# A decoder layer on one core: block products of the second MLP product alternate with tiles of the first, and weight sums are made by adding DMAs

## The chip, the core and the metric

The kernel runs on one core of one Trainium2 chip. The metric is the device time of one launch in microseconds (us), the median of the runs of a kernel; lower is better. Five engines work side by side: TensorE (PE, with its weight loads PEld), VectorE (DVE), ScalarE (ACT), GpSimd (POOL) and SyncE (SP), which here only issues DMAs. Each works through its own instructions in order; semaphores tie them together.

## What is computed

One layer over 512 positions of width 1024, in float32: a sparse attention branch and a latent attention branch, gates, an output projection, and then the MLP, which is all that the change touches:

```python
        x = x + merged @ w_out[l]
        h2 = rmsnorm(x, mlp_norm_g[l])
        x = x + jnp.square(jax.nn.relu(h2 @ w_ff1[l])) @ w_ff2[l]
    return rmsnorm(x, final_norm_g)
```

`w_ff1` is 1024 x 4096 and `w_ff2` 4096 x 1024.

## The kernel before, in words

Every float32 operand of a product is split in a high part `hi` (float32r, a Copy on ACT) and a rest `lo` (a subtraction on DVE); a product is three matmuls, hi·hi, lo·hi and hi·lo (`mm3`, L141 to L143).

**First product.** The 4096 hidden columns are cut into 32 tiles of 128. `ff1(f)` makes one tile for all 512 tokens: 8 x 3 = 24 matmuls of 512 columns into one PSUM bank, then Relu (L910) and Square (L911) on ACT into `z`. Its weights come from DRAM by SP (L112, tile `wraw`), and are split by `pre` (whi L119 on ACT, wlo L121 on DVE).

**Second product.** The hidden rows go in 8 groups `g` of 512, four ff1 tiles each. Within a group the product of z (transposed) and `w_ff2` is taken as a 2 x 2 block product in the manner of Strassen and Winograd, with seven block products in place of eight. The blocks A of z are 256 tokens by 256 hidden rows, the blocks B of the weights 256 hidden rows by 512 columns; S1 to S4 are sums of blocks of A, T1 to T4 sums of blocks of B. `ORDER` names the seven operand pairs and their order. One block product is a **pair** of units (m = 0, 1: 128 tokens each); a unit is 6 matmuls into one PSUM bank `pl` (four banks, `psL`), and then DVE adds the bank into `acc` (the result), `U` or `V` (sums that several blocks share), L979.

- The blocks B11, B12, B22, B21 of a group are loaded by SP into `wraw` (L918, `raws`), the same four buffers that the ff1 weights use.
- T1 to T4 (L944) and S1 to S4 (L929 to L935) are made on POOL, one tensor operation each.
- `put_a` splits an A operand into tile `as` (ACT L953, DVE L954), `put_b` a B operand into tile `b` (ACT L960, DVE L961), which has `NBS` = 6 buffers: a pair's buffer is free once its 12 matmuls are done, and `puts(g, k)` then fills it with the operand six pairs on.

**Order.** PE's order is that of the code. For each group it runs the four ff1 tiles of the next group in a row (21.8 us by the trace), and then the seven pairs of this group in a row. The other engines' instructions are placed by a scheduler. `finish` and `final` (L1001 to L1065) turn the sums of the last group into the output: sums on POOL and DVE, squares on ACT, the row factor `r` on POOL, and the scaled rows by ACT and DVE, in an order that `ff2` gives for the last group.

Of the kernel before, what the change touches and what calls it, by code (L numbers as in the profile page):

```python
# [49 lines left out]
def body(nc, tc, ctx, a, out, dbg=lambda name, ap: None):  # L50
    pe, dve, act, pool, sp = nc.tensor, nc.vector, nc.scalar, nc.gpsimd, nc.sync
# [19 lines left out]
    def utile(i, dt, name):  # L71
        return u_p.tile([128, 4, S], dt, tag=f"u{i}", name=name)
# [98 lines left out]
    k = 0  # L171
    for nk in (1, 1, 2, 2, 2):
# [3 lines left out]
        for kk in range(k, k + nk):  # L176
# [3 lines left out]
            else:  # L180
# [4 lines left out]
                                     op0=ALU.mult, op1=ALU.subtract)  # L185
            cs = [slice(128 * j, 128 * j + 128) for j in range(3)]
# [142 lines left out]
    for j in range(3):  # L329
# [9 lines left out]
        if j == 1:  # L339
# [12 lines left out]
            for j in range(2):  # L352
                t = t_p.tile([128, S], F32, tag="s2k", name="iqf", bufs=4)
# [523 lines left out]
    for b in range(NB):  # L877
# [10 lines left out]
    Z, AS, BS, RAW, TT, SS = {}, {}, {}, {}, {}, {}  # L890
# [21 lines left out]

    def raws(g):
        for key in ("B11", "B12", "B22", "B21"):
            j, n = int(key[1]) - 1, int(key[2]) - 1
            r = wr_p.tile([128, 1024], F32, tag="wraw", name="wraw").rearrange("p (q d) -> p q d", q=2)
            rows = slice((4 * g + 2 * j) * 128, (4 * g + 2 * j + 2) * 128)
            sp.dma_start(r, a["wff2"][rows, 512 * n:512 * n + 512].rearrange("(q p) d -> p q d", p=128))  # L918
            RAW[g, key] = r
# [18 lines left out]
    def operand_b(g, key):
        if key[0] == "B":
            return RAW[g, key]  # L940
        if (g, key) not in TT:
            t = TT[g, key] = wt_p.tile([128, 2, 512], F32, tag="t", name=key, bufs=3)
            x, y = {"T1": ("B12", "B11"), "T2": ("B22", "T1"), "T3": ("B22", "B12"), "T4": ("B21", "T2")}[key]
# [12 lines left out]

    def put_b(g, k):
        x = operand_b(g, ORDER[k][1])
        t = bs_p.tile([128, 2, 2, 512], F32R, tag="b", name="b", bufs=NBS)
        act.activation(t[:, 0], x, AF.Copy)  # L960
        dve.tensor_tensor(t[:, 1], x, t[:, 0].bitcast(F32), op=ALU.subtract)  # L961
        BS[g, k] = (t[:, 0], t[:, 1])

    BLOCK = {0: (0, 0), 3: (0, 1), 4: (0, 0), 5: (1, 1), 6: (1, 0)}

    def unit(g, k, m, cuts=(0, 512)):
        p = pl_tile()
        ah, al = AS[g, "op", k]
        bh, bl = BS[g, k]
        ms = slice(m * 128, (m + 1) * 128)  # L970
        for lo, hi in zip(cuts, cuts[1:]):
            c = slice(lo, hi)
            mm3(p[:, c], [(ah[:, q, ms], al[:, q, ms], bh[:, q, c], bl[:, q, c]) for q in range(2)])
            i, n = BLOCK.get(k, (0, 0))
            b = 2 * i + m
            cs = slice(512 * n + lo, 512 * n + hi)

            def add(t):
                dve.tensor_tensor(t, p[:, c], t, op=ALU.add)  # L979

            def first(t):
                if g == 0:
                    act.activation(t, p, AF.Copy)
                else:
                    add(t)

            if k in BLOCK:
                add(acc[:, b, cs])
            if k == 0:
                first(U[:, m])  # L990
            elif k == 1:
                add(U[:, m])
            elif k == 2:
                first(V[:, m])
            if g == NG - 1:
                finish(k, m, b, n, cs)

    def finish(k, m, b, n, cs):
        c12, c21, c22 = acc[:, m, 512:], acc[:, 2 + m, :512], acc[:, 2 + m, 512:]
        if k == 1:  # L1000
            pool.tensor_tensor(c21, c21, U[:, m], op=ALU.add)  # L1001
        elif k == 2:
            pool.tensor_tensor(V[:, m], U[:, m], V[:, m], op=ALU.add)  # L1003
            pool.tensor_tensor(c12, c12, V[:, m], op=ALU.add)  # L1004
        elif k == 5:
            pool.tensor_tensor(c21, c21, c22, op=ALU.add)
            dve.tensor_tensor(c22, c22, V[:, m], op=ALU.add)  # L1007
        if k >= 3:
            final(b, n, cs)

    def puts(g, k):
        n = NP * g + k + NBS
        if n < NP * NG:
            put_b(*divmod(n, NP))
        if g + 1 < NG and (k % 2 or k == NP - 1):
            for kk in range(k - k % 2, min(k - k % 2 + 2, NP)):
                put_a(g + 1, kk)

    def ff2(g):
        if g + 1 < NG:  # L1020
            raws(g + 1)
        if g < NG - 1:
            for k in range(NP):
                for m in range(2):
                    unit(g, k, m)
                puts(g, k)
        else:
            for k in range(NP - NBS):
                for m in range(2):
                    unit(g, k, m)  # L1030
                puts(g, k)
            for m in range(2):
                for k in range(NP - NBS, NP):
                    unit(g, k, m, (0, 256, 512) if m and k == NP - 1 else (0, 512))
# [57 lines left out]
    for g in range(NG):  # L1092
        if g + 1 < NG:
            for j in range(4):
                ff1(4 * (g + 1) + j)
        if g == NG - 2:
            uo = [utile(4 + i, F32, f"o{i}") for i in range(4)]
            fo = [uo[b // 2][:, 2 * (b % 2):2 * (b % 2) + 2].rearrange("p a b -> p (a b)") for b in range(NB)]
            gf = uo[2][:, 0:2].rearrange("p a b -> p (a b)")
            xf = [uo[2][:, 2], uo[2][:, 3], uo[3][:, 0], uo[3][:, 1]]  # L1100
            sp.dma_start(gf, bc(a["gfin"], [128, D]))
# [49 lines left out]
```

## Time and profile before

| | before |
|---|---|
| median of 3 runs | 749.47 us (748.76 to 751.18) |
| the profiled execution's own time | 748.43 us |
| its span, first to last instruction | 746.7 us |
| mean granted TensorE clock | 0.982 |
| busy: PE, DVE, ACT, POOL | 93%, 74%, 49%, 40% |

A row of the timeline gives the start, the duration, the engine, the line, the operation with its tiles, and, in brackets, how long the engine had stood idle and what released it. Matmuls follow each other every 0.227 us at full clock although each lasts 0.39, since they overlap; how fast PE goes is therefore read from starts. A stretch is described by the busy time of each engine in it. The MLP takes from about 371 us to the end of the span.

### The profile page before, as it was taken

To read this page: it belongs to the slowest core of one execution; us is meant where nothing else is said; L and a number is where in the kernel's file an instruction comes from. 1 tells how busy PE (TensorE), PEld (TensorE's weight loads), DVE (VectorE), ACT (ScalarE), POOL (GpSimd) and SP (SyncE) were. 2 spreads that over 40 slices of the span, in tenths; PEclk is the share of its full clock that TensorE was granted. 3 is DMA by queue.
4 is the path that set the end of the run, shared out by engine and by line. 5 is a ranking of instruction groups with operands and counts; after the bars stand their busy time and mean duration, and the time that the engine had idled before them with its cause. 6 is when DMAs were issued, how large, how long until landed. Compare 5 with 4: busy or idle time off the path is not lost. (4 is left out here: it accounts for less than half of the span.)

```text
span 746.7 us, 10090 instructions
## 1 busy us (share of the span) xinstructions
PE 696.4 (93%) x3653; PEld 559.2 (75%) x3654; DVE 555.1 (74%) x920; ACT 364.0 (49%) x630; POOL 301.2 (40%) x276
## 2 busy tenths in 40 slices
PE   9999999999999999999989989898998989989791
PEld 7879788678666678888878868686776868768571
DVE  6587899999999746753387775949679395892985
ACT  5566777645545455621265634435344353443332
POOL 2314596743355412300434615225151351534544
PEclk9999999999999999999999999999999999999996
DMA  8532531122311159830052231332322314221003
GB/s 312 208 107 86 148 114 43 43 85 84 115 43 44 44 174 334 285 110 0 1 198 86 85 114 57 106 98 78 116 84 85 112 56 141 84 85 57 0 1 113
DMA packets 30050, 77.18 MB, mean 103 GB/s; under 512 B 3568, under 2 KB 4464, under 8 KB 30000
## 3 DMA queue, kind: packets, MB, share of 16 engines
q1 hardware_dynamic: 29136, 75.45, 30.4%
q10 hardware_dynamic: 864, 1.08, 0.4%
q8 instruction: 29, 0.48, 0.3%
q14 instruction: 21, 0.17, 0.1%
HBM read 69.31 MB, written 6.29 MB: 101 GB/s over the span
## 5 line engine op out<-in xcount | busy, mean ns | idle before, releaser
L121 DVE TENSOR_TENSOR wlo<-wraw,whi 128x1024 fp32r<-128x1024 f32 (+1 forms) x60 | 86.0, 1437 | 56.8 <-ACT whi L119 56.1
L141 PE MATMUL pl<-b,as 128*128 128x512 f32 (+1 forms) x226 | 91.2, 404 | 34.2 <-DVE acc L979 26.5
L119 ACT ACTIVATE whi<-wraw 128x1024 fp32r<-128x1024 f32 (+1 forms) x71 | 74.7, 1052 | 98.4 <-PE pl L142 61.3
L143 PE MATMUL pl<-h2h,wlo 128*128 128x512 f32 (+1 forms) x280 | 104.7, 374 | 2.9 <-DVE wlo L121 2.9
L141 PE MATMUL pl<-h2h,whi 128*128 128x512 f32 (+1 forms) x280 | 104.9, 375 | 0.3 <-ACT h2h L874 0.3
L142 PE MATMUL pl<-h2l,whi 128*128 128x512 f32 (+1 forms) x280 | 104.6, 373 | 0.3 <-DVE h2l L875 0.3
L143 PE MATMUL pl<-b,as 128*128 128x512 f32 (+1 forms) x226 | 90.0, 398 | 0.0
L142 PE MATMUL pl<-b,as 128*128 128x512 f32 (+1 forms) x226 | 89.5, 396 | 0.0
L944 POOL TENSOR_TENSOR T<-wraw 128x1024 f32<-128x1024 f32 x16 | 42.2, 2634 | 101.2 <-DMA wraw<-wff 101.2
L979 DVE TENSOR_TENSOR acc<-pl,acc 128x512 f32<-128x512 f32 (+1 forms) x81 | 52.4, 674 | 40.0 <-PE pl L143 37.0
L141 PEld LDWEIGHTS pl<-b,as 128*128 128x128 f32 x226 | 43.7, 193 | 49.2 <-ACT as L953 17.8
L143 PEld LDWEIGHTS pl<-h2h,wlo 128*128 128x128 f32 x280 | 53.1, 190 | 12.5 <-DVE wlo L121 3.3
L142 PEld LDWEIGHTS pl<-h2l,whi 128*128 128x128 f32 x280 | 53.3, 190 | 9.9 <-DVE h2l L875 0.5
L141 PEld LDWEIGHTS pl<-h2h,whi 128*128 128x128 f32 x280 | 53.3, 190 | 9.8 <-ACT h2h L874 0.5
L944 POOL TENSOR_TENSOR T<-wraw,T 128x1024 f32<-128x1024 f32 x16 | 42.5, 2654 | 42.1 <-DVE b L961 24.0
L960 ACT ACTIVATE b<-T 128x1024 fp32r<-128x1024 f32 x32 | 33.7, 1057 | 45.2 <-PE pl L143 44.9
L143 PEld LDWEIGHTS pl<-b,as 128*128 128x128 f32 x226 | 43.6, 193 | 9.2
L142 PEld LDWEIGHTS pl<-b,as 128*128 128x128 f32 x226 | 43.8, 194 | 8.7
L714 DVE TENSOR_SCALAR oh<-posbc,thr 128x400 bf16<-128x400 f32 (+31 forms) x128 | 46.1, 412 | 3.5 <-PE pl L735 3.5
L595 POOL TENSOR_SCALAR pra<-pra,rs 128x400 f32<-128x400 f32 (+31 forms) x32 | 34.4, 1082 | 35.2 <-DVE rs L594 35.1
L237 PE MATMUL pl<-hh,whi 128*128 128x512 f32 x112 | 44.7, 399 | 0.0
L961 DVE TENSOR_TENSOR b<-wraw,b 128x1024 fp32r<-128x1024 f32 x24 | 43.2, 1802 | 1.4 <-ACT b L960 1.2
(307 smaller groups left out, 1654.5 us busy)
## 6 DMA issues: line engine op xcount, KB each, us to landing
wraw<-wff SPq DMA_DIRECT2D x64, 512.0 KB, 3.6
wraw<-wF SPq DMA_DIRECT2D x24, 512.0 KB, 3.3
gd<-gt SPq DMA_DIRECT2D x16, 256.0 KB, 2.2
wraw<-wbr SPq DMA_DIRECT2D x8, 512.0 KB, 4.2
wraw<-wout SPq DMA_DIRECT2D x8, 512.0 KB, 5.7
gx<-gd SPq DMA_DIRECT2D x16, 256.0 KB, 3.2
xtok<-x SPq DMA_DIRECT2D x4, 512.0 KB, 10.9
acc<-x SPq DMA_DIRECT2D x1, 2048.0 KB, 9.5
```

What stands on the lines that cost most here:

```text
L119: act.activation(hi, raw, AF.Copy)
L121: eng.tensor_tensor(lo, raw, hi.bitcast(F32), op=ALU.subtract)
L141: pe.matmul(ps, lh, rh, start=(i == 0), stop=False)
L142: pe.matmul(ps, lh, rl, start=False, stop=False)
L143: pe.matmul(ps, ll, rh, start=False, stop=(i == n - 1))
L237: pe.matmul(p, h[:, k], hh[k], start=(k == 0), stop=False)
L595: pool.tensor_scalar(pr, pr, rs, None, op0=ALU.mult)
L714: dve.tensor_scalar(oh[:, :n], posbc[:, :n], thr[:, 4 * G + q:4 * G + q + 1], None, op0=ALU.is_le)
L944: pool.tensor_tensor(t, operand_b(g, x), operand_b(g, y), op=ALU.subtract)
L960: act.activation(t[:, 0], x, AF.Copy)
L961: dve.tensor_tensor(t[:, 1], x, t[:, 0].bitcast(F32), op=ALU.subtract)
L979: dve.tensor_tensor(t, p[:, c], t, op=ALU.add)
```

## The change

**PE's order.** In a group the seven pairs are no longer in a row. Where a digit is a pair and a letter an ff1 tile of the next group, the order is now `0 a 1 2 b 3 4 c 5 d 6`. The ff1 tiles use the two banks of `psT` (`pt`), so the four banks of `psL` are left to the pairs. The operand pairs stand in another order (A12·B21 is second, S3·T3 sixth), and U gets its second part from pair 3.

**Weight sums.** T1 to T4 are not made by POOL's arithmetic. SP loads one source block from DRAM into the tile, and then POOL issues a second DMA that adds the other block to it (`accum_op`), from DRAM for T1 and T3, from the tile of T3 or T2 for T2 and T4. So that only additions are needed, the T's have other signs, and so have S1, S4 and the sums in `unit` and `finish`. The blocks B11, B21, B22 that are used as they are go into their own tile `raw` (3 buffers), T into `t` (3 buffers) and `b` has 5 buffers.

**Placement of the rest.** `load(g + 1, i)` comes after pair i, `put_b` five pairs ahead, `put_a` of the next group's first operand after tile b, of the next five after tile d, of the last after pair 6. In the last group pairs 0 and 1 run whole, then units 2 to 6 for m = 0, then for m = 1. The scaling of the final gain is on ACT.

```diff
-    ORDER = (("A11", "B11"), ("S2", "T2"), ("S1", "T1"), ("S4", "B22"), ("A12", "B21"), ("S3", "T3"),
+    ORDER = (("A11", "B11"), ("A12", "B21"), ("S1", "T1"), ("S2", "T2"), ("S4", "B22"), ("S3", "T3"),
              ("A22", "T4"))
-    NBS = 6
+    NBS = 5
...
-            p = pl_tile()
+            p = pt_tile().rearrange("p a b -> p (a b)")
             ff1_mm(p, f)
...
+    def raw(g, key):
+        r = RAW[g, key] = wt_p.tile([128, 2, 512], F32, tag="raw", name=key, bufs=3)
+        sp.dma_start(r, wsrc(g, key))
+
+    def tsum(g, key):
+        t = TT[g, key] = wt_p.tile([128, 2, 512], F32, tag="t", name=key, bufs=3)
+        x, y = {"T1": ("B11", "B12"), "T3": ("B12", "B22"), "T2": ("B11", "T3"), "T4": ("B21", "T2")}[key]
+        sp.dma_start(t, wsrc(g, x))
+        pool.dma_start(t, TT[g, y] if y[0] == "T" else wsrc(g, y), accum_op=ALU.add)
+
+    LOADS = ((raw, "B11"), (raw, "B21"), (tsum, "T1"), (tsum, "T3"), (tsum, "T2"), (raw, "B22"), (tsum, "T4"))
...
-                pool.tensor_tensor(t, z0[:, :, t1], z1[:, :, t1], op=ALU.add)
+                pool.tensor_tensor(t, z0[:, :, t1], z1[:, :, t1], op=ALU.subtract)
...
-            pool.tensor_tensor(t, operand_b(g, x), operand_b(g, y), op=ALU.subtract)
...
+    def pair(g, k):
+        for m in range(2):
+            unit(g, k, m)
         n = NP * g + k + NBS
         if n < NP * NG:
             put_b(*divmod(n, NP))
...
+    def group(g):
+        for step in "0a1 2b3 4c5 d6 ":
+            if step.isdigit():
+                pair(g, int(step))
+                load(g + 1, int(step))
+            elif step != " ":
+                ff1(4 * (g + 1) + "abcd".index(step))
+            if step == "b":
+                put_a(g + 1, 0)
+            if step == "d":
+                for k in range(1, 6):
+                    put_a(g + 1, k)
+        put_a(g + 1, 6)
+
+    def last_group(g):
+        for k in range(2):
+            pair(g, k)
+        for m in range(2):
+            for k in range(2, NP):
+                unit(g, k, m, (0, 256, 512) if m and k == NP - 1 else (0, 512))
...
-            pool.tensor_scalar(gf, gf, float(D) ** 0.5, None, op0=ALU.mult)
+    act.activation(gf, gf, AF.Copy, scale=float(D) ** 0.5)
```

In the rows below a name with a number is one tile: S_5930 one of the S, T_5967 one of the T, z_5871 the second half of a group's z. First POOL, around the sums S of one middle group. Before, two weight sums, three S, the third weight sum, the fourth S and the last weight sum:

```order
L944 TENSOR_TENSOR T_5552<-wraw 128x1024
L944 TENSOR_TENSOR T_5551<-wraw,T_5552 128x1024
L929 TENSOR_TENSOR S_5530<-z_5373,z_5440 128x512
L931 TENSOR_TENSOR S_5529<-S_5530,z_5373 128x512
L935 TENSOR_TENSOR S_5580<-z_5440,S_5529 128x512
L944 TENSOR_TENSOR T_5645<-wraw 128x1024
L933 TENSOR_TENSOR S_5625<-z_5373 128x512
L944 TENSOR_TENSOR T_5813<-wraw,T_5551 128x1024
```

Now, with T3, T2 and T4 of this group and T1 of the next group (T_6070) ahead of the four S of this group:

```order
L927 DMA T_5815<-wff 128x2x512
L927 DMA T_5837<-T_5815 128x1024
L927 DMA T_5967<-T_5837 128x1024
L927 DMA T_6070<-wff 128x2x512
L944 TENSOR_TENSOR S_5931<-z_5714,z_5871 128x512
L946 TENSOR_TENSOR S_5935<-S_5931,z_5714 128x512
```

The four tensor operations T became four DMA issues, and the last of them, which belongs to the group after, stands ahead of the S that this group's third pair needs.

Second DVE at the same place, where a group's operands are split while its first pair runs. Before, `as` pairs stand between the additions of single block products:

```order
L979 TENSOR_TENSOR acc<-pl,acc 128x512 x2
L961 TENSOR_TENSOR b<-T_5552,b 128x1024
L954 TENSOR_TENSOR as<-S_5530,as 128x512
L954 TENSOR_TENSOR as<-S_5580,as 128x512
L979 TENSOR_TENSOR acc<-pl,acc 128x512 x2
```

Now (pair 6 of the group before is added around S_5931, pair 0 of this group after all five):

```order
L960 TENSOR_TENSOR as<-z_5871,as 128x512
L960 TENSOR_TENSOR as<-S_5931,as 128x512
L989 TENSOR_TENSOR acc<-pl,acc 128x512
L968 TENSOR_TENSOR b<-B_5893,b 128x1024
L960 TENSOR_TENSOR as<-S_5935,as 128x512
L960 TENSOR_TENSOR as<-S_5940,as 128x512
L960 TENSOR_TENSOR as<-S_5944,as 128x512
L960 TENSOR_TENSOR as<-z_5871,as 128x512
L989 TENSOR_TENSOR acc<-pl,acc 128x512
L995 TENSOR_TENSOR U<-pl,U 128x512
L989 TENSOR_TENSOR acc<-pl,acc 128x512
L995 TENSOR_TENSOR U<-pl,U 128x512
```

What empties the banks of pair 0 now stands behind the splits of S2, S4, S3 and A22.

## Rows read from the trace of the kernel before

**Rows 1.** The page: span and busy time of each engine.
```profile
span 746.7 us, 10090 instructions
PE 696.4 (93%) x3653; PEld 559.2 (75%) x3654; DVE 555.1 (74%) x920; ACT 364.0 (49%) x630; POOL 301.2 (40%) x276
```

**Rows 2.** Timeline of ACT: the Relu of two successive ff1 tiles, and the splits.
```profile
448.73 0.58 ACT L910 ACTIVATE z<-pl 128x512 f32<-128x512 f32 x1
449.33 0.63 ACT L911 ACTIVATE z<-z 128x512 f32<-128x512 f32 x1
...
454.17 0.58 ACT L910 ACTIVATE z<-pl 128x512 f32<-128x512 f32 x1
...
464.31 1.06 ACT L960 ACTIVATE b<-wraw 128x1024 fp32r<-128x1024 f32 x1 [1.60 <-PE pl L143]
465.27 0.61 ACT L953 ACTIVATE as<-z 128x512 fp32r<-128x512 f32 x1
```

**Rows 3.** Stretches: from:to and length, busy time (count) of each engine, clock, DMA share, GB/s.
```profile
432.45:478.79 46.34, 43.01 (x181) 34.81 (x181) 33.07 (x35) 19.67 (x26) 15.99 (x8) 0.96 0.28 91
478.79:523.49 44.70, 41.37 (x181) 33.63 (x181) 33.04 (x35) 19.67 (x26) 16.37 (x8) 1.00 0.29 94
...
659.22:705.64 46.42, 41.35 (x180) 33.62 (x181) 32.59 (x33) 17.05 (x23) 21.42 (x9) 1.00 0.16 57
```

**Rows 4.** Timeline of PE, the rows where it had stood idle, and one more start.
```profile
384.40 0.50 PE L143 MATMUL pl<-h2h,wlo 128*128 128x512 f32 x1 [2.90 <-DVE wlo L121]
...
432.45 0.50 PE L141 MATMUL pl<-b,as 128*128 128x512 f32 x1 [3.09 <-DVE acc L979]
...
478.79 0.47 PE L141 MATMUL pl<-b,as 128*128 128x512 f32 x1 [2.57 <-DVE acc L979]
...
705.64 0.47 PE L141 MATMUL pl<-b,as 128*128 128x512 f32 x1 [2.58 <-DVE acc L979]
...
710.05 0.40 PE L141 MATMUL pl<-b,as 128*128 128x512 f32 x1
```

**Rows 5.** Timeline of DVE in the pairs of one group.
```profile
465.40 3.20 DVE L961 TENSOR_TENSOR b<-wraw,b 128x1024 fp32r<-128x1024 f32 x1 [0.20 <-ACT b L960]
468.53 0.68 DVE L954 TENSOR_TENSOR as<-z,as 128x512 fp32r<-128x512 f32 x1
...
473.44 1.21 DVE L961 TENSOR_TENSOR b<-T,b 128x1024 fp32r<-128x1024 f32 x1
474.58 3.46 DVE L954 TENSOR_TENSOR as<-S,as 128x512 fp32r<-128x512 f32 x2
477.96 1.28 DVE L979 TENSOR_TENSOR acc<-pl,acc 128x512 f32<-128x512 f32 x2
```

**Rows 6.** Timeline of POOL in the same group.
```profile
461.58 1.31 POOL L931 TENSOR_TENSOR S<-S,z 128x512 f32<-128x512 f32 x1
...
465.13 2.39 POOL L944 TENSOR_TENSOR T<-wraw 128x1024 f32<-128x1024 f32 x1
469.95 1.29 POOL L933 TENSOR_TENSOR S<-z 128x512 f32<-128x512 f32 x1 [2.43 <-DVE as L954]
474.73 2.76 POOL L944 TENSOR_TENSOR T<-wraw,T 128x1024 f32<-128x1024 f32 x1 [3.49 <-DVE b L961]
```

**Rows 7.** The page: DMA issues, with count, size and median us to landing.
```profile
wraw<-wff SPq DMA_DIRECT2D x64, 512.0 KB, 3.6
...
xtok<-x SPq DMA_DIRECT2D x4, 512.0 KB, 10.9
acc<-x SPq DMA_DIRECT2D x1, 2048.0 KB, 9.5
```

**Rows 8.** Timeline of DVE and POOL in the last group.
```profile
684.74 2.78 POOL L1102 TENSOR_SCALAR o<-o 128x1024 f32<-128x1024 f32 x1 [10.25 <-DMA o<-gfin]
...
713.62 0.68 DVE L979 TENSOR_TENSOR acc<-pl,acc 128x512 f32<-128x512 f32 x1
...
740.28 0.42 DVE L979 TENSOR_TENSOR acc<-pl,acc 128x256 f32<-128x256 f32 x1 [0.70 <-PE pl L143]
```

More of the change, by code (lines that the diff above doesn't have):

```diff
@@ L911, in ff1, with wsrc, load @@
         act.activation(z, z, AF.Square)
[L913 to L919, printed above, removed]
+    def wsrc(g, key):
+        j, n = int(key[1]) - 1, int(key[2]) - 1
+        rows = slice((4 * g + 2 * j) * 128, (4 * g + 2 * j + 2) * 128)
+        return a["wff2"][rows, 512 * n:512 * n + 512].rearrange("(q p) d -> p q d", p=128)
+    def raw(g, key):
[7 more added lines that the diff above has]
+    LOADS = ((raw, "B11"), (raw, "B21"), (tsum, "T1"), (tsum, "T3"), (tsum, "T2"), (raw, "B22"), (tsum, "T4"))
+    def load(g, i):
+        if g < NG:
+            f, key = LOADS[i]
+            f(g, key)
     def operand_a(g, key):
-        z0, z1 = Z[g, 0], Z[g, 1]
+        z0, z1 = Z.get((g, 0)), Z.get((g, 1))
         t0, t1 = slice(0, 256), slice(256, 512)
@@ L934, in operand_a @@
             else:
-                pool.tensor_tensor(t, z1[:, :, t0], operand_a(g, "S2"), op=ALU.subtract)
+                pool.tensor_tensor(t, z1[:, :, t0], operand_a(g, "S2"), op=ALU.add)
         return SS[g, key]
[L938 to L943, printed above, removed]
-            pool.tensor_tensor(t, operand_b(g, x), operand_b(g, y), op=ALU.subtract)
-        return TT[g, key]
     def put_a(g, k):
@@ L957, in put_b @@
     def put_b(g, k):
-        x = operand_b(g, ORDER[k][1])
+        key = ORDER[k][1]
+        x = (RAW if key[0] == "B" else TT)[g, key]
         t = bs_p.tile([128, 2, 2, 512], F32R, tag="b", name="b", bufs=NBS)
@@ L962, in put_b @@
         BS[g, k] = (t[:, 0], t[:, 1])
-    BLOCK = {0: (0, 0), 3: (0, 1), 4: (0, 0), 5: (1, 1), 6: (1, 0)}
+    BLOCK = {0: (0, 0), 1: (0, 0), 4: (0, 1), 5: (1, 1), 6: (1, 0)}
     def unit(g, k, m, cuts=(0, 512)):
@@ L976, in unit @@
             cs = slice(512 * n + lo, 512 * n + hi)
[L978 to L983, printed above, removed]
-                else:
[L985 to L994, printed above, removed]
+            if k in BLOCK:
+                t = acc[:, b, cs]
+                if k == 5:
+                    dve.tensor_tensor(t, t, p[:, c], op=ALU.subtract)
+                else:
+                    dve.tensor_tensor(t, p[:, c], t, op=ALU.add)
+            t = {0: U, 2: V, 3: U}.get(k)
+            if t is not None:
+                if g == 0 and k != 3:
+                    act.activation(t[:, m], p, AF.Copy)
+                else:
+                    dve.tensor_tensor(t[:, m], p[:, c], t[:, m], op=ALU.add)
             if g == NG - 1:
@@ L999, in finish @@
         c12, c21, c22 = acc[:, m, 512:], acc[:, 2 + m, :512], acc[:, 2 + m, 512:]
-        if k == 1:
+        if k == 3:
             pool.tensor_tensor(c21, c21, U[:, m], op=ALU.add)
-        elif k == 2:
-            pool.tensor_tensor(V[:, m], U[:, m], V[:, m], op=ALU.add)
-            pool.tensor_tensor(c12, c12, V[:, m], op=ALU.add)
+            pool.tensor_tensor(V[:, m], U[:, m], V[:, m], op=ALU.subtract)
+            pool.tensor_tensor(c12, c12, V[:, m], op=ALU.subtract)
         elif k == 5:
-            pool.tensor_tensor(c21, c21, c22, op=ALU.add)
-            dve.tensor_tensor(c22, c22, V[:, m], op=ALU.add)
-        if k >= 3:
+            pool.tensor_tensor(c21, c21, c22, op=ALU.subtract)
+            dve.tensor_tensor(c22, c22, V[:, m], op=ALU.subtract)
+        if k in (1, 4, 5, 6):
             final(b, n, cs)
-    def puts(g, k):
+    def pair(g, k):
+        for m in range(2):
+            unit(g, k, m)
         n = NP * g + k + NBS
@@ L1014, in puts @@
             put_b(*divmod(n, NP))
[L1015 to L1034, printed above, removed]
+    def group(g):
[17 more added lines that the diff above has]
+                unit(g, k, m, (0, 256, 512) if m and k == NP - 1 else (0, 512))
     parts = {b: 0 for b in range(NB)}
@@ L1083, in body @@
     V = z_p.tile([128, 2, 512], F32, name="V")
-    pool.tensor_tensor(acc[:, 2:4, :512], acc[:, 2:4, :512], acc[:, 2:4, 512:], op=ALU.subtract)
-    raws(0)
+    pool.tensor_tensor(acc[:, 2:4, :512], acc[:, 2:4, :512], acc[:, 2:4, 512:], op=ALU.add)
+    for i in range(NP):
+        load(0, i)
     for j in range(4):
@@ L1091, in body @@
             put_b(0, k)
[L1092 to L1101, printed above, removed]
-            pool.tensor_scalar(gf, gf, float(D) ** 0.5, None, op0=ALU.mult)
-        ff2(g)
+    for g in range(NG - 1):
+        group(g)
+    uo = [utile(4 + i, F32, f"o{i}") for i in range(4)]
+    fo = [uo[b // 2][:, 2 * (b % 2):2 * (b % 2) + 2].rearrange("p a b -> p (a b)") for b in range(NB)]
+    gf = uo[2][:, 0:2].rearrange("p a b -> p (a b)")
+    xf = [uo[2][:, 2], uo[2][:, 3], uo[3][:, 0], uo[3][:, 1]]
+    sp.dma_start(gf, bc(a["gfin"], [128, D]))
+    act.activation(gf, gf, AF.Copy, scale=float(D) ** 0.5)
+    last_group(NG - 1)
     ff_st.close()
```

## The prediction, made before the changed kernel had run

> **What bounds the kernel now.** I read the page first: PE is busy 93% of a span of 746.7 us [rows 1], but busy time of overlapping matmuls hides gaps, so I took PE's pace from starts. The Relu of two successive ff1 tiles starts 5.44 us apart [rows 2], which is 24 matmuls at 0.227 us. A pair, 12 matmuls, is then 2.72 us, and a group of four tiles and seven pairs 4 x 5.44 + 7 x 2.72 = 40.8 us. Next the stretches from one long idle of PE to the next: there are six of one group each between 432.45 and 705.64 us, two of 46.3 us, one of 46.4 and three of 44.7 (three stand there) [rows 3]. The difference is lost time, and the idle rows of PE say who ends it: DVE's additions into `acc` [rows 4]. In the seven pairs in a row a pair needs a bank every 1.36 us, and DVE has 33 us of work per group [rows 3], most of it there: splits of `b` at 1.2 us that stretch to 3.2 while POOL works on T, and pairs of `as` splits that take 3.46 in place of 1.28 [rows 5, 6]. The bound is DVE's queue within the pairs, not its 33 us in 40.8. After a long idle of PE the clock falls in some groups: 0.96 mean beside 1.00, and the stretch is 46.3 in place of 44.7 [rows 3].
>
> Against the work at 0.227 us per matmul, the profiled execution loses, to the start of the last group:
> - From the late `wlo` of ff1 tile 3 to 432.45 [rows 4]: the wait ends at 384.40 and is 2.90 long, so work would go on at 381.50. It holds 22 matmuls of the tile, four tiles and six pairs, 5.0 + 21.8 + 16.3 = 43.1 of 50.95: **7.9 lost**.
> - The six groups: 705.64 − 432.45 = 273.2 for 6 x 40.8 = 244.8: **28.4 lost**.
> - The last pair of group 6, 705.64 to 710.05 at the low clock: 4.4 for 2.7, **1.7 lost**.
>
> Together 38.0. The last group takes the rest, from 710.05 to the end: 36.7.
>
> **What the change does to each term.** *Interleaving.* Two pairs in a row are now the longest run; between them PE has 5.44 us in `pt` banks, which ACT empties. In a group DVE adds 16 banks, 0.64 each, splits seven `b` (1.21) and seven `as` (0.68) and four weights (about 1.2): 10.2 + 8.5 + 4.8 + 4.8 = 28.3 of 40.8 [rows 5]. Per pair it is at most four additions and one split, 3.8, with tiles between. So the 28.4 and the 1.7 go, unless something new is late. Its place can be read in the order: DVE splits S1, S2, S4, S3 and A22 ahead of the additions of pair 0, and pair 2 needs pair 0's banks. That is the new edge.
>
> *How long that edge holds.* Let t = 0 be the start of pair 0. The last tile of z is done at −2.72, Relu and Square bring z to −1.5 [rows 2]. If POOL begins S1 at s, S1, S2, S4 and S3 follow at 1.3 each, and take turns with DVE's splits where both read from memory [rows 5, 6]; after two such turns the last S ends near s + 7.1, its split on ACT and DVE and that of A22 (0.6 + 0.7 + 0.7) near s + 9.6, the first bank of pair 0 is free 1.3 later, at s + 10.9. Pair 2 is due at 2.72 + 5.44 + 2.72 = 10.9. So s may be 0 without loss, and from there every microsecond is PE's.
>
> *What sets s.* T1 of the next group is added by a DMA that POOL issues ahead of S1. Its buffer was T2's, which T4 reads. So: `put_b` of T1 runs after pair 4, which ends at −16.3, and its DVE half ends at −14.0 (1.06 + 1.21) [rows 2, 5]; SP's load for T4, 3.6 [rows 7], lands at −10.4; the add takes X, from POOL's issue to landing; SP's load for T1, 3.6, lands at X − 3.2 − 3.6 = X − 6.8; POOL issues the add, about 1.0. Hence s = X − 5.8, not under −1.5.
>
> *X.* The trace has no DMA from POOL and none that adds. Nearest rows: a plain load of 512 KB lands after 3.6, one of 2 MB after 9.5 [rows 7]. That is 1.97 per 512 KB and 1.6 fixed. An add has the old contents to read as well, so I count 512 KB twice: 1.6 + 3.9 = 5.5, and 0.5 for POOL's issue and for other loads in flight: **X = 6.0**. Below, 3.6 (the add for nothing); above, 9.5 to 10.9, the slowest rows of that view. The Trainium skill, in DMA: Bandwidth & Descriptors, Anatomy of one DMA — SWDGE (gpsimd) path, fits a POOL DMA by 2.0 us plus bytes over 436 GB/s, and Collectives: The Full Stack, The bandwidth ceiling, says that an adding DMA is slow not for the addition but for its two source reads; by both, X would be an estimated 2.0 + 2 x 1.2 = 4.4, and the sum below 6 us lower. No run here shows that.
>
> With X = 6.0, s = 0.2; I add 0.8, since four further DMAs of 512 KB per group make loads land later than 3.6: **1.0 per group, six groups, 6.0**.
>
> There is a second loop: `put_b` of T3 waits for those additions; then load 3.6, add X, the add of T2, the add of T4, load 3.6, issue 1.0, and from s to the end of `put_b` of T3 10.9 + 1.3 + 1.2 = 13.4. That is 21.6 + 3X, and exceeds 40.8 from X = 6.4 on. From there a group costs 3 us for every microsecond of X.
>
> *T sums off POOL.* Four operations, 2.4 to 2.8 each [rows 6], leave POOL; what they hid behind was DVE, and they return what they took from it (3.2 against 1.21). This is inside the 28.4 already.
>
> *Start.* ff1 weights no longer share buffers with B, so tile 3 does not wait for `wlo`, and group 0 is interleaved as well: the 7.9 go. New: ACT's split of T2 stands ahead of z's last Square, and T2 needs two adds in a row. The loads begin near 371; T3's, the fourth, lands near 371 + 1.6 + 4 x 1.97 = 380.5, so with X = 6 T2 is there at 392.5. Its split (1.06 and 1.21), the Square and A12's split (0.63, 0.61, 0.68) take 4.2, to 396.7, and pair 1 is due at 381.5 + 5.44 + 2.72 + 5.44 = 395.1. I count **1.5**, and 2 per microsecond of X.
>
> *Last group.* Its additions began at 713.62, 3.6 after its first matmul [rows 8], and DVE and POOL, not PE, set the rest. Now they begin at s + 9.6, and the scaling of the gain, now on ACT, stands ahead of z's last Square; POOL got that gain after 10.25 of waiting at 684.74 [rows 8], a microsecond after the last tile. So they begin some 6 later, and one `b` split more (1.2) falls in; the units of m = 1 are one fewer after the two whole pairs, from which I take 3 back: **4.4 longer**, with bounds 1 and 8.
>
> **Sum.** 748.4 − 38.0 + 6.0 + 1.5 + 4.4 = 722.3 for the profiled execution; the median of the runs is 1.0 above it, so 723.3, rounded to **723**.
>
> **Rivals.**
> - *A cheap add.* X is 3.6 to 5: no edge is reached, start and groups lose nothing, the last group's additions begin 1.5 sooner: 749.5 − 38.0 + 2.9 = 714. For it: POOL's queue is nearly empty. Against: it would read as cheap as a plain load.
> - *Half a gain.* X is 7 to 8.2, the second loop binds at 21.6 + 3 x 7.4 = 43.8, 3.0 per group: 749.5 − 38.0 + 18 + 4.3 + 4.4 = 738.
> - *Slower: the chain of adds paces the groups.* Three adds in a row and two loads stand in the second loop. It costs as much as the 38.0 when six groups cost 38.0 − 5.5 − 4.4 = 28.1, 4.7 each: 45.5 = 21.6 + 3X, X = 8.0. With X = 9.5 a group is 50.1, and the time 749.5 − 38.0 + 6 x 9.3 + 8.5 + 4.4 = 780. For it: T stretches from 2.4 to 2.8 when DVE reads memory too [rows 6], and POOL may be held up as much when it writes a DMA's descriptors. The Trainium skill, SBUF — State Buffer, SBUF: two separate sides, warns of that: a DMA issued by POOL waits while DVE holds the shared port; but it says so of DVE's two-port modes, and the same page (Who interferes with whom) gives tensor_tensor none, which is all that DVE runs here. Hence a small chance.
> - *The order undone.* POOL could wait at T1's add so long that alternation brings nothing. That is the same edge, at s = 4: a group of 44.8, and 746.
>
> **How the numbers follow.** About 0.3% (2.2 us) is what a measurement can tell from no change. Forecast (X 5 to 7, 716 to 733) 0.50; cheap add 0.14; half a gain 0.15; the chain paces 0.17; ends within 2.2 us of now, by any of these, 0.04. Faster 0.79, same 0.04, slower 0.17. The range leaves out half of the cheap cases and most of the slow ones: 712 to 748.
>
> **What would show it.** Right: PE's starts 40.8 to 43 apart per group, with the only idle rows ahead of pair 2, ended by DVE; S1 within 2 us after z; landing of POOL's DMAs near 6; no idle at tile 3; no T on POOL. Wrong: landing above 8, POOL standing at its DMA issues, groups over 45; or idle of PE at other pairs; or a last group over 45 us.

## The result, and the profile after

The changed kernel takes 761.3 us (median of 4 runs, 759.15 to 762.06) beside 749.1 before: a ratio of 1.016, 95% interval 1.012 to 1.020. It is slower; 723, between 712 and 748, had been forecast. The profiled execution took 762.06 us. Its page, against [rows 1] and [rows 7]:

```profile
span 760.3 us, 10231 instructions
PE 701.6 (92%) x3653; PEld 563.8 (74%) x3654; DVE 520.7 (68%) x920; ACT 366.1 (48%) x631; POOL 252.8 (33%) x275
...
wraw<-wff SPq DMA_DIRECT2D x32, 512.0 KB, 4.5
T<-wff SPq DMA_DIRECT2D x32, 512.0 KB, 4.5
...
B<-wff SPq DMA_DIRECT2D x24, 512.0 KB, 6.4
T<-wff POOLq DMA_DIRECT2D x16, 512.0 KB, 7.6
T<-T POOLq DMA_DIRECT2D x16, 512.0 KB, 5.0
```

DVE and POOL have 34 and 48 us less to do, and the kernel is longer all the same. PE's rows with idle time ahead of them, against [rows 4] (two later ones of the last group are left out):

```profile
405.13 0.79 PE L141 MATMUL pl<-b,as 128*128 128x512 f32 x1 [11.02 <-ACT as L959]
408.29 0.79 PE L143 MATMUL pl<-b,as 128*128 128x512 f32 x1 [1.94 <-DVE as L960]
457.27 0.47 PE L141 MATMUL pl<-b,as 128*128 128x512 f32 x1 [3.21 <-ACT z L911]
503.71 0.76 PE L141 MATMUL pl<-b,as 128*128 128x512 f32 x1 [3.76 <-ACT z L911]
549.67 0.53 PE L141 MATMUL pl<-b,as 128*128 128x512 f32 x1 [2.41 <-ACT z L911]
595.36 0.47 PE L141 MATMUL pl<-b,as 128*128 128x512 f32 x1 [2.99 <-ACT z L911]
640.33 0.77 PE L141 MATMUL pl<-b,as 128*128 128x512 f32 x1 [3.90 <-ACT z L911]
685.80 0.47 PE L141 MATMUL pl<-b,as 128*128 128x512 f32 x1 [1.95 <-ACT z L911]
...
728.02 0.77 PE L141 MATMUL pl<-b,as 128*128 128x512 f32 x1 [4.73 <-DVE U L995]
```

The first two belong to pair 1 of the first group; each of the others stands ahead of pair 2 of a group. The Relu that six of them name ends beside DVE's first addition into U (595.22 and 595.21 in the group of 595.36; the addition is the first row of DVE below); by the program the first unit of pair 2 waits for that addition, which frees its bank. From one such wait to the next (columns as in [rows 3]):

```profile
405.13:457.27 52.14, 46.99 (x192) 37.88 (x193) 35.83 (x39) 27.09 (x39) 17.52 (x13) 0.92 0.71 187
...
549.67:595.36 45.69, 42.70 (x180) 34.88 (x181) 29.19 (x35) 19.90 (x27) 10.64 (x8) 0.96 0.65 173
595.36:640.33 44.97, 41.07 (x181) 33.71 (x181) 29.21 (x35) 19.91 (x27) 10.66 (x8) 0.98 0.68 176
640.33:685.80 45.47, 43.52 (x181) 35.48 (x181) 29.19 (x35) 19.89 (x27) 10.65 (x8) 0.94 0.55 139
```

The DMA share of a group went from 0.16 to 0.31 up to 0.55 to 0.71. In the terms of the prediction, against PE's work at full clock: 457.27 − 381.5 = 75.8 for 56.7 (22 matmuls, a group, a tile, two pairs), 19.1 lost; five groups, 228.5 for 204.0, 24.5 lost; from 685.80 to 717.44, where the last group begins, 31.6 for 29.9, 1.7 lost; the last group 42.9 in place of 36.7. That is 45.3 in place of 38.0, and 6.2: 748.4 + 7.3 + 6.2 = 761.9.

**What paces a group.** For the group that begins at 595.36: DVE's first addition into U and its splits of T3, in this group and in the next; POOL's rows; then landing times, each from the DMA view of a stretch that holds its issue alone (the adds of T3, T2 and T4, and SP's load of the next T1):

```profile
594.54 0.67 DVE L995 TENSOR_TENSOR U<-pl,U 128x512 f32<-128x512 f32 x1
...
596.34 1.21 DVE L968 TENSOR_TENSOR b<-T,b 128x1024 fp32r<-128x1024 f32 x1
...
641.30 1.21 DVE L968 TENSOR_TENSOR b<-T,b 128x1024 fp32r<-128x1024 f32 x1
```

```profile
601.61 1.21 POOL L927 DMA_DIRECT2D T<-wff  x1 [9.95 <-DVE V L995]
611.61 0.90 POOL L927 DMA_DIRECT2D T<-T  x1 [8.79 <-DVE b L968]
619.81 0.86 POOL L927 DMA_DIRECT2D T<-T  x1 [7.30 <-DMA T<-T]
628.78 1.21 POOL L927 DMA_DIRECT2D T<-wff  x1 [8.10 <-DMA T<-wff]
629.52 1.79 POOL L944 TENSOR_TENSOR S<-z,z 128x512 f32<-128x512 f32 x1
```

```profile
T<-wff POOLq DMA_DIRECT2D x1, 512.0 KB, 9.4
...
T<-T POOLq DMA_DIRECT2D x1, 512.0 KB, 7.6
...
T<-T POOLq DMA_DIRECT2D x1, 512.0 KB, 4.5
...
T<-wff SPq DMA_DIRECT2D x1, 512.0 KB, 3.8
```

From the split of T3 (DVE, ends at 597.55): the load of the next T3 into the buffer that this split has read, 3.5, at 601.61 its add, 9.4, at 611.61 T2's add, 7.6, at 619.81 T4's add, 4.5, at 624.44 the load of the next T1, 3.8, S1 at 629.52, pair 2 at 640.33, and the next split of T3 ends at 642.51. The ring closes in 44.96 us, the length of the group (44.97). From each landing to POOL's next issue pass about 0.6 us.

Of the five groups from 457.27 to 685.80 this is the only one in which T2's add is the last thing that T4's add waits for. In the other four it is T4's own load. POOL's row names it in two of them, of which this is one, and in the other two the load landed 1.3 after T2's add:

```profile
483.15 0.86 POOL L927 DMA_DIRECT2D T<-T  x1 [9.07 <-DMA T<-wff]
```

That load fills T1's old buffer, which T1's split frees after pair 4. So a second chain, with PE's own work in it, is as long as the ring: pairs 2, 3 and 4, T1's split, T4's load (5.9 and 5.2 where its landing is recorded), T4's add, the next T1's load, S1, pair 2. T1's split ended 16.2 after pair 2 had begun in the group of 595.36, and 17.8 to 18.7 in the other four, whose mean clock was 0.94 to 0.96 beside 0.98. Both chains end in the same piece: T4's add, the load of the next T1 into the buffer that this add has read, S1.

The three adds of the ring lie in stretches with these DMA shares (last but one column):

```profile
601.60:611.00 9.40, 9.40 (x43) 7.80 (x42) 7.82 (x11) 4.94 (x6) 1.21 (x1) 1.00 0.91 244
611.60:619.20 7.60, 7.60 (x35) 6.31 (x34) 2.51 (x3) 2.18 (x3) 0.90 (x1) 1.00 0.94 223
619.80:624.30 4.50, 4.50 (x22) 3.72 (x21) 1.79 (x2) 2.16 (x4) 0.86 (x1) 1.00 0.66 134
```

The slow adds fall where the DMA engines are full, the quick one where they are not.

**The start.** T1's and T3's adds were issued from 379.35 on and landed after 9.9 and 11.3 (median 10.6); T2's, issued at 392.14, after 9.9. ACT stood with T2's split and, behind it, z's last Square:

```profile
391.21 0.58 ACT L911 ACTIVATE z<-pt 128x512 f32<-128x512 f32 x1
402.04 1.06 ACT L967 ACTIVATE b<-T 128x1024 fp32r<-128x1024 f32 x1 [10.25 <-DMA T<-T]
403.00 0.61 ACT L912 ACTIVATE z<-z 128x512 f32<-128x512 f32 x1
```

### The profile page after: what moved, and what is told of

It is laid out like the page before. It is cut to its first block, busy times and chain, and to the rows that moved or that the text cites. A ratio compares the mean times of both kernels' runs of the same rounds, so it can differ in the third digit from the quotient of the medians.

```text
span 760.3 us, 10231 instructions
## 1 busy us (share of the span) xinstructions
PE 701.6 (92%) x3653; PEld 563.8 (74%) x3654; DVE 520.7 (68%) x920; ACT 366.1 (48%) x631; POOL 252.8 (33%) x275
## 3 DMA queue, kind: packets, MB, share of 16 engines
q1 hardware_dynamic: 35664, 88.04, 34.7%
q0 software_dynamic: 6656, 16.78, 12.7%
## 4 chain that ended last, share of the span: by engine, by line
PE 50%; DVE 18%; DMA 17%; POOL 5%; ACT 5%; issue 4%; SPq 0%; POOLq 0%; DVEq 0%; ACTq 0%
DMA T<-wff 8%; DMA T<-T 7%; PE pl L141 6%; PE pl L143 6%; PE pl L142 6%; PE pl L237 3%; PE pl L238 3%; PE pl L239 3%; DVE b L968 3%; PE pt L141 2%; PE pt L142 2%; PE pt L143 2%; DVE nmx L590 2%; DVE oh L714 2%; DVE as L960 2%
## 5 line engine op out<-in xcount | busy, mean ns | idle before, releaser
L141 PE MATMUL pl<-b,as 128*128 128x512 f32 (+1 forms) x226 | 94.7, 419 | 42.5 <-ACT z L911 18.2
L141 PE MATMUL pt<-h2h,whi 128*128 128x512 f32 x232 | 90.3, 389 | 0.0
L142 PE MATMUL pt<-h2l,whi 128*128 128x512 f32 x232 | 90.3, 389 | 0.0
L143 PE MATMUL pt<-h2h,wlo 128*128 128x512 f32 x232 | 90.3, 389 | 0.0
L927 POOL DMA_DIRECT2D T<-wff x16 | 19.6, 1239 | 129.5 <-DMA T<-wff 60.8
L927 POOL DMA_DIRECT2D T<-T x16 | 14.1, 880 | 129.2 <-DMA T<-wff 60.3
L968 DVE TENSOR_TENSOR b<-T,b 128x1024 fp32r<-128x1024 f32 x32 | 39.7, 1240 | 24.6 <-ACT b L967 24.6
L960 DVE TENSOR_TENSOR as<-S,as 128x512 fp32r<-128x512 f32 x32 | 33.4, 1081 | 29.7 <-ACT as L959 29.5
L141 PEld LDWEIGHTS pt<-h2h,whi 128*128 128x128 f32 x232 | 43.8, 189 | 9.2
L142 PEld LDWEIGHTS pt<-h2l,whi 128*128 128x128 f32 x232 | 43.6, 188 | 9.2
L143 PEld LDWEIGHTS pt<-h2h,wlo 128*128 128x128 f32 x232 | 43.6, 188 | 9.1
L714 DVE TENSOR_SCALAR oh<-posbc,thr 128x400 bf16<-128x400 f32 (+31 forms) x128 | 45.7, 410 | 3.8 <-PE pl L735 3.6
L989 DVE TENSOR_TENSOR acc<-pl,acc 128x512 f32<-128x512 f32 (+1 forms) x65 | 42.4, 671 | 7.8 <-PE pl L143 4.5
```

The source lines that it names most:

```text
L141: pe.matmul(ps, lh, rh, start=(i == 0), stop=False)
L142: pe.matmul(ps, lh, rl, start=False, stop=False)
L143: pe.matmul(ps, ll, rh, start=False, stop=(i == n - 1))
L714: dve.tensor_scalar(oh[:, :n], posbc[:, :n], thr[:, 4 * G + q:4 * G + q + 1], None, op0=ALU.is_le)
L927: pool.dma_start(t, TT[g, y] if y[0] == "T" else wsrc(g, y), accum_op=ALU.add)
```

## The experiments

Theory A: the ring of adding DMAs paces the groups, and two of them in a row the start. e1 and e3 each undo one half of the change, e5 both; e2 and e4 cut into the ring.

**e1: interleaved, sums by POOL.**

```diff
-        pool.dma_start(t, TT[g, y] if y[0] == "T" else wsrc(g, y), accum_op=ALU.add)
+        if y[0] == "T":
+            v = TT[g, y]
+        else:
+            v = wt_p.tile([128, 2, 512], F32, tag="v", name="v" + key, bufs=1)
+            sp.dma_start(v, wsrc(g, y))
+        pool.tensor_tensor(t, t, v, op=ALU.add)
```

> Interleaving kept, T sums back on POOL's arithmetic: POOL adds into the loaded tile, and what an adding DMA took from DRAM SP now loads into one extra buffer (raw has 2 buffers to make room). Theory A (the chain of adding DMAs paces the groups: load 4.0, add of T3 9.4, of T2 7.6, of T4 4.5, load of T1 3.8, S1, and 13 from S1 to the next load of T3, 45.0 in all; and T2's two adds in a row cost the start): with POOL sums of about 2.6 the chain is 4.0 + 3 x 2.6 + 3.8 + 1.3 + 13 = 30, under the 40.8 of PE's work. Groups of 41 to 42.5 instead of 45.7, PE's wait of 11 us before pair 1 of the first group gone, the last group as now: 762 - 6 x 3.5 - 13 = 728, between 720 and 735. Theory B (the interleaved order itself costs: S2, S4, S3 and A22 are split on DVE ahead of pair 0's additions whoever makes T): groups stay at 45 or more, 748 to 760. A price against A: POOL's sums stretch DVE's splits, 1.2 to 3.2, which could give back up to 2 us per group.

Measured 741.5 us, ratio 0.990 (0.987 to 0.992). The groups are 42.55, just above what A expected (41 to 42.5); the total is outside its range, since the start lost 11 as well (450.93 − 381.5 = 69.4 for 56.7, less a group's 1.75). There POOL's sums of T took up to 3.25 and DVE's splits beside POOL's sums 2.28 to 3.18, and PE waited 0.66, 3.63 and 2.09, with a clock of 0.87 over that stretch. In the groups 1.5 is left, and its place is the edge from S1 to pair 2: T1's sum stands ahead of S1 (POOL), and pair 2 starts 10.75 after S1 (last row, PE).

```profile
479.40 3.37 POOL L932 TENSOR_TENSOR T<-T,vT 128x1024 f32<-128x1024 f32 x1 [4.78 <-DMA T<-wff]
482.73 1.73 POOL L949 TENSOR_TENSOR S<-z,z 128x512 f32<-128x512 f32 x1
...
493.48 0.47 PE L141 MATMUL pl<-b,as 128*128 128x512 f32 x1 [1.50 <-ACT z L911]
```

**e2: a fourth buffer for T.**

```diff
-        r = RAW[g, key] = wt_p.tile([128, 2, 512], F32, tag="raw", name=key, bufs=3)
+        r = RAW[g, key] = wt_p.tile([128, 2, 512], F32, tag="raw", name=key, bufs=2)
-        t = TT[g, key] = wt_p.tile([128, 2, 512], F32, tag="t", name=key, bufs=3)
+        t = TT[g, key] = wt_p.tile([128, 2, 512], F32, tag="t", name=key, bufs=4)
```

> A fourth buffer for T, paid with one of raw. T3's load no longer waits for put_b of T3 of the group before but for T4's add, and stands, with T1's, ahead of S1 on POOL. Theory A: the loop that ran through S1 and put_b of T3 is cut; the loop left is 13.4 + 4.0 (load of T2) + 7.6 + 0.7 + 4.6 + 3.8 + 1.3 = 35, under 40.8: groups of 41 to 42.5, start unchanged: 762 - 6 x 4 = 738, between 732 and 745. Theory B: no change, 757 to 765. Theory C (the DMA engines are too full: adding DMAs get slower the more of them overlap): the loop has slack, but adds take 10 or more, groups of 44 or more, 752 to 765.

740.7 us, ratio 0.990 (0.986 to 0.994), within A's range. Five groups take 41.5 to 43.3, 42.35 in the mean: the ring through T3's split is cut, as A has it, but not all that holds S1. POOL now issues the add of the next T3 0.75 ahead of S1 (527.80 and 528.55 in one group), and PE still waits 0.4 to 2.3 ahead of pair 2. By the page adds from DRAM land after 7.2 and from tile to tile after 7.1, where the changed kernel has 7.6 and 5.0; the second kind is slower, as C has it, and yet the groups stay under C's 44.

**e3: the order undone, adding DMAs kept.**

```diff
     def group(g):
-        for step in "0a1 2b3 4c5 d6 ":
...
+        for j in range(4):
+            ff1(4 * (g + 1) + j)
+        for k in range(NP):
+            pair(g, k)
+            load(g + 1, k)
+            if k % 2 or k == NP - 1:
+                for kk in range(k - k % 2, k + 1):
+                    put_a(g + 1, kk)
```

> The adding DMAs kept, the interleaving undone: four ff1 tiles of the next group in a row, then the seven pairs, operands of the next group split after pairs 1, 3, 5 and 6. Theory A: here S1 of a group is made a whole run of tiles before it is used, and T's adds have 22 us more, so no chain of DMAs reaches PE; what is left is DVE's queue within the seven pairs, as before the change, less what POOL's sums took from it: groups of 42.5 to 45.5, no 11 us wait in the first group, 738 to 752. Theory B (adds harmless, interleaving harmful): the same 738 to 752. Theory C (DMA load slows everything): over 755.

733.5 us, ratio 0.979 (0.976 to 0.982): better than any theory said. Every group before the last is at PE's pace, with a DMA share of 0.72 in the one shown, and with seven pairs in a row:

```profile
508.41:549.24 40.83, 40.83 (x182) 33.75 (x181) 26.89 (x34) 19.57 (x28) 10.26 (x8) 1.00 0.72 193
```

So the groups reach PE's pace without the interleaving, which was expected to bring it. The start is bad here too: ACT stands for T2, the Relu of tile 4 behind it, and PE waits 15.9 us for a bank.

**e4: copies in place of adds.**

```diff
-        pool.dma_start(t, TT[g, y] if y[0] == "T" else wsrc(g, y), accum_op=ALU.add)
+        pool.dma_start(t, TT[g, y] if y[0] == "T" else wsrc(g, y))
```

> POOL's second DMA of each T copies instead of adding, so T holds only its second summand and the output is of another sum; everything else is as in the changed kernel. Theory A with the price in the two reads of an add: landing falls from 7.6 (DRAM) and 5.0 (tile to tile) to 4 to 5 and 3 to 4, the chain is 4.0 + 4.5 + 4 + 0.7 + 3.5 + 3.8 + 1.3 + 13 = 35, groups of 41 to 42.5, the first wait halved: 730 to 742. If the price lies in POOL's issue or in its queue, not in the adding: landings as now, 757 to 765.

733.9 us (one run), within A's range; three groups in a row take 42.2 to 42.4; the first wait is 6.6 for 11.0. Landing times within the MLP fall from 6.8 to 5.0 (DRAM) and from 5.2 to 4.8 (tile to tile). SP's queue (q1) and POOL's (q0) on the page of the changed kernel, and POOL's on the page of this one (packets, MB, share of 16 engines):

```profile
q1 hardware_dynamic: 35664, 88.04, 34.7%
q0 software_dynamic: 6656, 16.78, 12.7%
```

```profile
q0 software_dynamic: 4608, 16.78, 6.4%
```

For the same bytes written an add holds the DMA engines twice as long as a copy: 12.7% of 760.3 us for 32 DMAs is 3.0 us of all 16 engines each. The Trainium skill (Collectives: The Full Stack, The bandwidth ceiling) says of the adds of a reduce-scatter, which DMAs make, that their price lies in two source reads and not in the addition. Twice the engine time agrees with that, though this run can't tell the second read from the addition itself. What is left of the wait, 1.1 to 1.4 per group, comes by the second chain: T4's load landed 1.3 and 2.9 after T2's copy in two of these groups (512.44 after 511.13, 597.11 after 594.24).

**e5: neither half.** e1's and e3's edits together: order undone, sums by POOL.

> Interleaving undone as in e3, and the T sums on POOL's arithmetic as in e1: of the change only the buffers, the banks of the tiles, the signs and the order of operands are left. It tells what made e3's groups take 40.8. Theory D (before the change PE stood because POOL's T sums stretched DVE's splits within the seven pairs, and the adding DMAs took that away): groups of 43 to 45, DVE's splits of b beside a T sum at 2 us or more, 745 to 755. Theory E (the separate buffers and banks did it): groups of 40.8 to 41.5, 725 to 737.

741.6 us, ratio 0.990 (0.987 to 0.994), groups of 43.1: theory D in the groups and the splits, though the total lies below D's range, and above E's. Beside POOL's sums DVE's splits take 2.6 and 2.2 again where they take 1.2 without, and PE waits 1.55 per group for an addition into `acc`:

```profile
512.34 1.21 DVE L973 TENSOR_TENSOR b<-T,b 128x1024 fp32r<-128x1024 f32 x1
...
515.88 2.62 DVE L973 TENSOR_TENSOR b<-B,b 128x1024 fp32r<-128x1024 f32 x1
...
519.62 2.23 DVE L973 TENSOR_TENSOR b<-B,b 128x1024 fp32r<-128x1024 f32 x1
```

| us: total, (group) | sums by POOL | sums by adding DMAs |
|---|---|---|
| seven pairs in a row | 741.6 (43.1) | 733.5 (40.8) |
| interleaved | 741.5 (42.55) | 761.3 (45.7) |

Neither half is slow; the two together are. The other 1.6 to 3.3 per group between the kernel before (44.7 to 46.4) and e5 lie in what all four share, the buffers, banks, placement and operand order; they were not taken apart.

**e6: e3 with another start.** In the first group T1 to T4 are sums by POOL of four blocks loaded once.

```diff
-    for i in range(NP):
-        load(0, i)
...
+        sp.dma_start(b12, wsrc(0, "B12"))
+        raw(0, "B22")
+        raw(0, "B11")
+        raw(0, "B21")
...
+        pool.tensor_tensor(TT[0, "T3"], b12, b22, op=ALU.add)
+        pool.tensor_tensor(TT[0, "T1"], b12, b11, op=ALU.add)
+        pool.tensor_tensor(TT[0, "T2"], TT[0, "T3"], b11, op=ALU.add)
...
+        pool.tensor_tensor(TT[0, "T4"], TT[0, "T2"], b21, op=ALU.add)
```

> e3 with another start: in the first group alone T1 to T4 are made by POOL's arithmetic from the four blocks B, loaded once each (4 loads of 512 KB in place of 7 loads and 4 adds). e3 lost 18.5 between 381.5 and the end of tile 7 (426.8 - 381.5 - 26.8), PE's wait of 15.9 among it, ended when ACT had T2 at last. Theory A: the waits of the start are T2's two adds in a row beside seven loads; with POOL's four sums in about 12 us from 377 on the start loses 2 to 5, the rest stays: 733.5 - 15 = 718, between 715 and 723. If ACT's order is the cause whoever makes T2 (its splits ahead of the Relu of tile 4): still 6 to 10 lost, 722 to 727.

725.4 us, ratio 0.969 (0.966 to 0.972): the second case of the two. The wait is 6.6, and ACT's rows tell why: four splits of S stand ahead of the Relu of tile 4, whichever way T is made.

```profile
395.43 0.63 ACT L959 ACTIVATE as<-S 128x512 fp32r<-128x512 f32 x1 [4.43 <-POOL S L944]
...
402.18 0.63 ACT L959 ACTIVATE as<-S 128x512 fp32r<-128x512 f32 x1 [1.29 <-POOL S L948]
402.71 0.58 ACT L911 ACTIVATE z<-pt 128x512 f32<-128x512 f32 x1
```

**e7: the changed kernel with that start.** The edit of e6 on the interleaved order.

> The changed kernel with the same start as in e6 and nothing else. The start lost about 14.7 by the stretches (13 of waits and the low clock after them); theory A: 761 - 10 to 13, as S1 to S4 of the first group still stand between the last T and pair 2: 747 to 752, groups still at 45 to 46. If the loss of the first group came from the interleaving and not from T2: 757 to 762.

745.0 us, ratio 0.996 (0.993 to 0.998), somewhat better than A's range. The groups stay at 45.0 in the mean. Two stretches that each hold one of PE's waits, the first at full clock, the second with the low clock behind its wait of 4.19:

```profile
473.98:517.49 43.51, 41.05 (x182) 33.72 (x181) 29.20 (x34) 19.91 (x28) 10.66 (x8) 1.00 0.68 179
517.49:565.19 47.70, 43.51 (x182) 35.47 (x181) 29.18 (x34) 19.88 (x27) 10.65 (x8) 0.93 0.64 168
```

The second holds the same matmuls, for which PE is busy 2.5 us longer. That is not lost as a whole: the next wait is only 2.54. Taken from pair 2 to pair 2, five groups are 43.55, 45.24, 46.05, 45.00 and 44.82, and S1 starts at the same distances within 0.02 (43.53, 45.26, 46.04, 45.00, 44.82). So it is S1, held back by T's chain, that paces the groups, and the clock can count only as far as it delays pair 4 and with it T1's split.

**e8: e7 with a buffer of its own for each T.** The one test that leaves the adds, their number and POOL's order alone and takes out the piece that both chains share: T1's load need no longer wait for T4's add (nor T4's load for T1's buffer).

```diff
-        r = RAW[g, key] = wt_p.tile([128, 2, 512], F32, tag="raw", name=key, bufs=3)
+        r = RAW[g, key] = wt_p.tile([128, 2, 512], F32, tag="raw", name=key, bufs=2)
...
-        t = TT[g, key] = wt_p.tile([128, 2, 512], F32, tag="t", name=key, bufs=3)
+        t = TT[g, key] = wt_p.tile([128, 2, 512], F32, tag=key, name=key, bufs=1)
```

> e7 (interleaved, adding DMAs, first group's T by POOL) with a buffer of its own for each of T1 to T4 (raw has 2). T1's load then waits for put_b of the old T1, long done, and no longer for the landing of T4's add; POOL's order of issues is the same, T1's still ahead of S1. Theory A: the loop loses T4's add and T1's load and is 13.4 + 4.0 + 9.4 + 0.7 + 7.6 + 1 = 36 from S1 to S1, under 40.8: S1 follows z at once, groups of 40.8 to 42 instead of 45.0, 745 - 6 x 3.6 = 723, between 719 and 730. If the pace of the groups has another cause (DVE's order, banks, load on the DMA engines): groups at 44 or more, 738 to 748.

724.1 us, ratio 0.968 (0.966 to 0.970). The groups are 40.8, with a DMA share of 0.75; T1's add is issued right behind T4's (POOL), and S1 waits for z alone. The adds from DRAM land after 8.4 here by the page, later than in the changed kernel (7.6), and cost the groups nothing.

```profile
489.90:530.70 40.80, 40.80 (x182) 33.78 (x181) 30.14 (x35) 20.13 (x27) 10.96 (x8) 1.00 0.75 193
```

```profile
549.86 0.86 POOL L927 DMA_DIRECT2D T<-T  x1 [6.28 <-DVE acc L987]
550.66 1.29 POOL L927 DMA_DIRECT2D T<-wff  x1
557.21 1.29 POOL L944 TENSOR_TENSOR S<-z,z 128x512 f32<-128x512 f32 x1 [5.26 <-ACT z L912]
```

**e9: e6, and T2 of the last group added by POOL.**

```diff
+        if g == NG - 1 and key == "T2":
+            pool.tensor_tensor(t, t, TT[g, y], op=ALU.add)
+            return
```

> e6 with one more edit in the last group alone: T2 is added by POOL's arithmetic and not by a DMA (5.7 us there), since PE waits 4.7 before the last group's third pair for additions that stand behind T2's split on DVE. Expected: that wait shrinks by about 3, 725.3 - 3 = 722, between 720 and 725; no change if PE's next wait (1.6 and 6.7 further on) takes it up: 724 to 727.

722.8 us, ratio 0.966 (0.964 to 0.969), the lowest time of all, though its interval overlaps those of e6 and e8, so the totals alone don't show the gain. The wait of 4.7 before the third pair became 1.4, and 0.55, 0.55 and 0.2 at later units; PE's next wait grew from 1.6 to 2.4.

## Why the prediction was wrong, step by step

- **What bounds the kernel before.** DVE's queue within the pairs ends PE's waits: right. But the cure was named wrongly. The seven pairs in a row lose nothing once DVE's splits keep their 1.2 us (e3, 40.8), and 2.3 per group with POOL's sums beside them (e5, 43.1). The step "this is inside the 28.4 already" passed over the fact that the weight sums could leave POOL, and the 28.4 go, without the interleaving (in the changed kernel's buffers and operand order). The Trainium skill (SBUF — State Buffer, Who interferes with whom) says that a DVE instruction with two SBUF inputs contends with a GpSimd instruction that reads SBUF. e5's rows agree (2.62 and 2.23 beside 1.21).
- **Interleaving frees PE from that queue.** Right as far as it went: with T's chain cut the groups are 40.8 (e8). It adds nothing to what the adding DMAs bring: e8 and e6 (0.968 and 0.969) can't be told apart.
- **The edge from S1 to pair 2**, 10.9 after S1 and PE's only wait in a group: right in place and size. S1 at 629.52, pair 2 at 640.33: 10.8; in e1 10.75.
- **X = 6.0.** This step failed. One price was taken for all adds, from loads in a kernel whose DMA engines were busy for 0.16 to 0.29 of a group [rows 3]. The adds and their loads raise that to 0.65, and while T3's and T2's adds run to 0.9: they took 9.4, 7.6 and 4.5. The sum should have counted the DMA engines' own time: 11 loads at 1.6 (34.7% of the span for the 88 MB of SP's queue) and 4 adds at 3.0 are 30 us in a group of 41, before any of it comes at once. The plain loads were priced too low in the same way: 3.6 for T4's load, which took 5.1 to 5.9. The estimate of 4.4 from the Trainium skill's figures (DMA: Bandwidth & Descriptors) fits only T4's add (4.5). That load on the engines is the cause of the late landings is borne out by the shares and by e4, where the engine time of an add halves; it is not shown, since no run changed the other loads alone. Two of the prediction's own signs of being wrong came true here, a landing above 8 and groups over 45.
- **The second loop, 21.6 + 3X.** Right as a mechanism: it is the ring above, and e8 opens it. With the mean of 7.2 it gives 43.1 where the ring took 44.96: beside the three adds it holds 23.5 and not 21.6, the loads being a little longer (3.5 and 3.8, where two of 3.6 were counted) and about 0.6 passing from each landing to the next issue, which the sum counted once. The mean of the five groups is 45.7, since in four of them the other chain, the one of "What sets s", was longer still: T4's load took more than 3.6, and the clock, 0.94 to 0.96 after PE's waits, put T1's split 1.6 to 2.5 later. The sum had neither. 31 us were lost in the groups (six times 4.9, and 1.7) where 6.0 were counted.
- **The start**, 1.5: 19.1 less one group's 4.9, that is 14.2. The adds took 10.6 and 9.9 where 6.0 each were counted, with four loads of 512 KB issued by SP around each of the two times (373.35 to 380.36, and 391.64 to 393.10). By the step's own rule, 1.5 and 2 per microsecond of X, that is an estimated 10. The other 4 were not taken apart; a second wait of 1.94 and a clock of 0.92 lie in this stretch. e7 gives most of the loss back (16 us less than the changed kernel, about 4 of them in the groups).
- **The last group**, 4.4 with bounds 1 and 8: 6.2.
- **The rivals.** "The order undone" described the groups: S1 at s = 4 and 44.8 per group. In the group above pair 1's last matmul starts at 636.04, so pair 0 began near 625.4, S1 came 4.1 later, and the group took 44.97. Its total of 746 fell short by about as much as the start was underpriced (14.2, not 1.5). "Half a gain" had X nearest (7 to 8.2), and "the chain of adds paces the groups" the ring and the sign, with a chance of 0.17; its turning point of X = 8.0 was too high, because the start was priced for X near 6 and the ring without the 1.9 above. The range left that case out.

Sum with what was measured: 748.4 − 38.0 + 31.1 + 14.2 + 6.2 = 761.9.

## What to carry to other kernels

A DMA in place of an engine's work took contention away here and added latency: before issuing one, follow its buffer round to its next use and write the ring down, and then look for a second chain through the same piece. Four adds in three buffers closed a ring of 45 us; a fourth buffer in common, which raw could spare, loosened it (42.35), and four buffers, one for each sum, opened it (40.8). Price a new DMA by the load that all of them together will make, not by rows from an idle queue. And where two changes come together, undo each alone, and both. The kernel with neither half takes 741.6 us; adding DMAs alone bring 8 us, the interleaving alone nothing in the total and 0.5 us per group, and the two together cost 20.

## What the runs showed of the hardware that was not expected

- An adding DMA of 512 KB from POOL holds the 16 DMA engines for 3.0 us, a copy half as long (12.7% and 6.4% of the span for 32 of them). In one group it landed after 4.5 us at a DMA share of 0.66, and after 7.6 and 9.4 at 0.94 and 0.91.
- A weight sum on POOL doubles the time of a DVE split beside it (1.2 to 2.6, e5). With adding DMAs in its place the same splits take 1.21, at a DMA share of 0.72 (e3).
- A wait of PE can cost a second time through the clock. In e7 the matmuls behind a wait of 4.19 first started every 0.43 us, the lower of the two levels (1.2 and 2.4 GHz), and a group's work took 43.51 of busy time in place of 41.05. The length of the wait alone does not tell: behind waits of 2.32, 2.46 and 2.54 the busy time stayed at 41.05 to 41.09, and behind another one of 2.54 it was 42.68.
